# A hybrid decoder layer on one core: gMLP and twelve column tiles moved to the front, there in pairs of seven block products

## The chip, the core and the metric

The kernel runs on one core of one Trainium2 chip. TensorE (PE) multiplies matrices into PSUM banks; VectorE (DVE), ScalarE (ACT) and GpSimd (POOL) work element by element; SyncE (SP) issues most of the DMAs, ScalarE some. Each engine works off its own instructions in the order of the program and waits at semaphores. The metric is the device time of one execution in microseconds; the kernel before takes 1228.83 us (median of 3 runs, 1227.72 to 1228.85).

## The reference, cut to what matters

x is 1024 tokens by 1024 channels, float32. Every mixer has four heads or groups, 256 channels wide.

```python
h = rmsnorm(x, norm_gain)
proj = h @ w_in                       # all inputs of all mixers and the merge gates
ys = (gated_deltanet(gdn_qkv, ..., gdn_z, ...),
      spatial_gating(sg_u, sg_v, sg_z, ...),       # gMLP
      rwkv7_time_mix(rw, rw_z, ...),
      native_sparse_attention(nsa_q, nsa_kv, ..., nsa_z, ...))
gates = jnp.split(jax.nn.sigmoid(merge), 4, axis=-1)
mixed = sum(gates[i] * (ys[i] @ w_branch[i]) for i in range(4))
return rmsnorm(x + mixed @ w_out, final_gain)
# in spatial_gating: u, v = gelu(u), gelu(v); v = layernorm over 64 channels;
# mixed = lower-triangular 128x128 position mixing of v per group; u * (mixed + b) * silu(z)
```

## The kernel before

The input projection is cut into column tiles of 128 output channels. The normalised input lies in SBUF as two parts, hh (rounded) and hl (the rest), all 1024 channels by 1024 tokens, with channels on partitions. A weight tile is loaded in two halves (wt, L1001), and each is split into wh (ScalarE, L1006) and wl (VectorE, L1008). A column tile (`col_tile`) has two halves of 512 tokens; for each, 8 steps over the channels by 3 products (hh·wh, hh·wl, hl·wh: L1023 to L1025), 24 matmuls a half and 48 a tile. The result leaves PSUM through ScalarE (L1034, or L1051 for a gate) and is parked in DRAM. These are called dense matmuls here.

The program is traced in this order: a first stage (rmsnorm, mixed with the tiles RW 6, 2, 3), the tiles RW 0, 1, 4, 5 and RWZ, a small projection (L1181 on), the rwkv mixer, tiles GD and GDZ, the gated delta mixer (`gdn`), tiles NK, NQ, NZ, the sparse attention (`nsa`), tiles GM 2, 3, 0, 1 and GMZ (gMLP's inputs and gate), the gMLP mixer (`gmlp`, L617), the 32 tiles of the merge gates, the merge (L1256 to L1258) and the output projection (L1287 to L1290) with the last norm. A scheduler at build time fixes each engine's order: work traced later fills the places where work traced earlier would wait, so column tiles that are traced behind a mixer stand between its instructions. Weight splits have high priority.

The mixers' results Y are read back from DRAM before the merge: sixteen loads (yr, L1236, two buffers), each split into yh (ScalarE, L1237) and yl (VectorE, L1238), in the order Y2, Y0, Y3, Y1 (rwkv, delta, attention, gMLP). Beside them the weights of the output projection are loaded (wot, L1223, two buffers) and split on ScalarE and POOL (L1225). The pool of these buffers shares SBUF space with the attention's pools.

gMLP works on halves of 512 tokens: gelu of v (VectorE L612 and L614), 16 transposes (L655), a layernorm (L660 to L667, with a power on POOL, L667), gelu of u (L612 on POOL), the scale (L676), 64 matmuls for the position mixing (L683), and two products (L685, L689).

Of the kernel before, what the change touches and what calls it, by code (L numbers as in the profile page):

```python
# [19 lines left out]
D = 1024  # L20
# [596 lines left out]
def gmlp(G, src, zs, y, ws, bs, lg, lb):  # L617
# [3 lines left out]
    with tc.tile_pool(name="gm", bufs=1, reuse_waits="tile") as P:  # L621
# [17 lines left out]
        def front(half):  # L639
# [4 lines left out]
            t = P.tile([128, 4, 512], F32, name="gmt")  # L644
# [3 lines left out]
            gelu2(nc, x[:, 2:4], t[:, 2:4], nc.vector.tensor_mul)  # L648
# [19 lines left out]
            gelu2(nc, x[:, 0:2], t[:, 0:2], nc.gpsimd.tensor_mul)  # L668
# [314 lines left out]
def body(tc, xT, x, w, wsm, rw_up, rw_cols, gd_conv, gd_hp, gd_gw, gm_ws, gm_bs, gm_lg, gm_lb,  # L983
# [4 lines left out]
    with ExitStack() as ctx:  # L988
        G = setup(tc, ctx)
        hpool = ctx.enter_context(tc.tile_pool(name="h", bufs=1))  # L990
        sp = ctx.enter_context(tc.tile_pool(name="stream", bufs=1))
# [7 lines left out]
        def load_w(src, k0, n):  # L999
            wt = sp.tile([128, 4, 128], F32, name="wt", bufs=3)  # L1000
            nc.sync.dma_start(wt[:, :, :n], src[:, k0:k0 + 4])  # L1001
            return wt

        def split_w(wt, eng=nc.gpsimd, pool=sp, bufs=3):
            wh = pool.tile([128, 4, 128], F32R, name="wh", bufs=bufs)
            nc.scalar.copy(wh, wt)  # L1006
            wl = pool.tile([128, 4, 128], F32R, name="wl", bufs=bufs)
            eng.tensor_sub(wl, wt, wh.bitcast(F32))  # L1008
            return wh, wl
# [18 lines left out]
        def stage():  # L1028
            return sp.tile([128, 512], F32, name="stg", bufs=4)
# [39 lines left out]
        with tc.tile_pool(name="xp", bufs=1) as XP:  # L1069
            banks = [[bank(G, tag, n) for _ in range(2)] for tag, n in (("st", 2), ("m", 2), ("sc", 3))]  # L1070

            def load_x(pc, a):
                if a == 0:
                    xs[pc] = XP.tile([128, 8, 256], F32, name="xt", bufs=3)
                ks = slice(4 * a, 4 * a + 4)
                nc.sync.dma_start(xs[pc][:, ks], xT.rearrange("k p t -> p k t")[:, ks, 256 * pc:256 * pc + 256])

            def stats(pc):

                xt = xs[pc]  # L1080
                s2 = XP.tile([128, 8, 256], F32, name="xsq", bufs=2)
                for a in range(2):
                    ks = slice(4 * a, 4 * a + 4)
                    nc.scalar.activation(s2[:, ks], xt[:, ks], AF.Square)
                    nc.vector.tensor_add(s2[:, 4 * a:4 * a + 2], s2[:, 4 * a:4 * a + 2], s2[:, 4 * a + 2:4 * a + 4])
                nc.vector.tensor_add(s2[:, 0:2], s2[:, 0:2], s2[:, 4:6])
                pss = bank(G, "sc", 3) if pc == 2 else bank(G, "acc", 1)
                for t in range(2):
                    for k in range(2):
                        nc.tensor.matmul(pss[:, t:t + 1], s2[:, k, 128 * t:128 * t + 128], one, start=(k == 0), stop=(k == 1))  # L1090
                rs = XP.tile([128, 2], F32, name="xrs", bufs=2)
                nc.vector.tensor_scalar(rs, pss[:, 0:2], 1.0 / D, 1e-6, op0=OP.mult, op1=OP.add)
                nc.gpsimd.tensor_tensor(rs, rs, G.mhalf[:, 0:2], op=OP.pow)
                return rs, pss[:, 256:512]

            def spread(rs, pb):

                with tc.issue_after(after.ins):
                    for t in range(2):
                        nc.tensor.transpose(pb[:, 128 * t:128 * t + 128], rs[:, t:t + 1].to_broadcast([128, 128]), G.ident)  # L1100
                return pb

            def apply(pc, rb):
                xt, sl = xs[pc], slice(256 * pc, 256 * pc + 256)
                for k in range(8):
                    nc.vector.scalar_tensor_tensor(xt[:, k], xt[:, k], gn[:, k:k + 1], rb, op0=OP.mult, op1=OP.mult)
                    nc.scalar.copy(hh[:, k, sl], xt[:, k])
                    (nc.gpsimd if k % 3 == 1 else nc.vector).tensor_sub(hl[:, k, sl], xt[:, k], hh[:, k, sl].bitcast(F32))

            def products(pc, ks, j, parts):  # L1110
                sl = slice(256 * pc, 256 * pc + 256)
                p = banks[j][pc // 2][:, 256 * (pc % 2):256 * (pc % 2) + 256]
                for k in ks:
                    wh, wl = w0[j][k // 4]
                    for n in parts:
                        a, b = ((wh, hh), (wh, hl), (wl, hh))[n]
# [256 lines left out]
```

## Time and profile before

| | us |
|---|---|
| median of the runs | 1228.83 |
| the profiled execution | 1225.36 |
| its span in the trace | 1223.6 |
| TensorE busy in it | 1168.8 (96%) |
| VectorE | 816.5 (67%) |
| ScalarE | 539.0 (44%) |
| GpSimd | 176.8 (14%) |

The span is the traced execution from its first to its last instruction, on the profile's own clock; the execution's device time has a little around it. Engines overlap, so the shares are not a sum. Matmuls are pipelined: one is listed with some 0.4 us, but the next starts after 0.23 us. Some matmul records are missing from the trace.

### The profile page before, as it was taken

The numbers are of one execution on the slowest core, as the hardware profiler recorded it, in microseconds if no ns is written. First come the engines' busy times: TensorE is split into PE (matmuls) and PEld (weight loads), VectorE is DVE, ScalarE is ACT, GpSimd is POOL, SyncE is SP. The second block draws the span as 40 slices with busy tenths as digits, with TensorE's granted clock in tenths as the row PEclk, the third lists the DMA queues.
The fourth block names the chain that finished last, engine by engine and source line by source line (L and its number), as shares of the span: only waits on it lengthen the run. The fifth ranks groups of instructions, "written<-read, shape, count | busy, mean of one in ns | idle before, by whom it ended". The sixth has DMA issues, their size and how long they took to land. (4 is left out here: it accounts for less than half of the span.)

```text
span 1223.6 us, 18178 instructions
## 1 busy us (share of the span) xinstructions
PE 1168.8 (96%) x6214; PEld 948.3 (78%) x6214; DVE 816.5 (67%) x2309; ACT 539.0 (44%) x1366; POOL 176.8 (14%) x158
## 2 busy tenths in 40 slices
PE   7999999998999999989999999999999999999997
PEld 6888777786777777877777887777787778888886
DVE  7612699778574868969765798888867431788122
ACT  6422454454333465575554565556554342221222
POOL 5320000100002000001000000000003220675510
PEclk9999999999999999999999999999999999999999
DMA  6222443121322553323323322212125563676223
GB/s 219 78 103 86 145 133 118 61 74 35 108 79 70 121 170 99 105 82 102 110 80 126 127 78 65 66 52 69 45 69 189 180 225 112 230 243 216 95 86 129
DMA packets 113105, 140.11 MB, mean 115 GB/s; under 512 B 36544, under 2 KB 59968, under 8 KB 112884
## 3 DMA queue, kind: packets, MB, share of 16 engines
q1 hardware_dynamic: 95588, 107.22, 27.9%
q10 hardware_dynamic: 17424, 31.73, 7.1%
q8 instruction: 49, 0.80, 0.3%
q14 instruction: 44, 0.36, 0.1%
HBM read 94.78 MB, written 44.12 MB: 114 GB/s over the span
## 5 line engine op out<-in xcount | busy, mean ns | idle before, releaser
L1023 PE MATMUL st<-hh,wh 128*128 128x512 f32 x944 | 380.4, 403 | 2.3 <-ACT stg L1051 2.3
L1024 PE MATMUL st<-hh,wl 128*128 128x512 f32 x944 | 379.4, 402 | 0.0
L1025 PE MATMUL st<-hl,wh 128*128 128x512 f32 x944 | 377.2, 400 | 0.0
L1023 PEld LDWEIGHTS st<-hh,wh 128*128 128x128 f32 x944 | 178.7, 189 | 35.9 <-ACT stg L1051 3.6
L1025 PEld LDWEIGHTS st<-hl,wh 128*128 128x128 f32 x944 | 178.4, 189 | 32.7 <-issue 1.0
L1024 PEld LDWEIGHTS st<-hh,wl 128*128 128x128 f32 x944 | 178.5, 189 | 32.3 <-issue 1.9
L1008 DVE TENSOR_TENSOR wl<-wt,wh 128x512 fp32r<-128x512 f32 x134 | 99.0, 740 | 96.4 <-ACT wh L1006 94.3
L1006 ACT CAST wh<-wt 128x512 fp32r<-128x512 f32 x140 | 86.3, 618 | 113.3 <-PE st L1025 103.8
L917 ACT ACTIVATE P<-sc,m 128x512 f32<-128x512 f32 (+3 forms) x80 | 44.8, 563 | 30.7 <-DVE m L912 19.5
L1051 ACT ACTIVATE stg<-st 128x512 f32<-128x512 f32 x64 | 38.1, 595 | 41.6 <-PE st L1025 41.4
L102 DVE TENSOR_TENSOR invP<-invX,invL 128x16 f32<-128x16 f32 (+18 forms) x240 | 53.9, 259 | 0.3
L105 DVE TENSOR_REDUCE invX<-invP 128x8 f32<-128x240 f32 (+18 forms) x240 | 52.7, 252 | 0.2
L1287 PE MATMUL sc<-woh,hh 128*128 128x512 f32 x128 | 49.8, 389 | 0.0
L1288 PE MATMUL sc<-wol,hh 128*128 128x512 f32 x128 | 49.8, 389 | 0.0
L1293 DVE TENSOR_TENSOR o<-sc,xr 128x512 f32<-128x512 f32 x16 | 11.1, 692 | 56.1 <-PE sc L1290 56.1
L1264 POOL TENSOR_TENSOR mx<-mx,stg 128x512 f32<-128x512 f32 x28 | 38.6, 1379 | 60.2 <-DVE stg L1263 59.1
L912 DVE TENSOR_REDUCE m<-sc 128x1 f32<-128x512 f32 (+3 forms) x80 | 41.2, 532 | 0.6 <-PE sc L837 0.2
L1034 ACT COPY stg<-st 128x512 f32<-128x512 f32 x39 | 22.9, 587 | 39.9 <-PE st L1025 35.7
L1270 ACT CAST hh<-mx 128x512 fp32r<-128x512 f32 x16 | 9.9, 622 | 62.6 <-POOL mx L1264 54.8
L30 POOL IOTA tril<- 128x128 f32 x1 | 0.2, 248 | 234.6 <-PE sc L837 234.6
L259 POOL MEMSET sv<- 64x512 f32 x8 | 4.2, 519 | 201.0 <-ACT O L297 162.4
L1295 ACT ACTIVATE jk<-o 128x512 f32<-128x512 f32 x16 | 10.1, 631 | 51.6 <-DVE o L1293 51.6
(458 smaller groups left out, 2386.7 us busy)
## 6 DMA issues: line engine op xcount, KB each, us to landing
wt<-in_w_dram SPq DMA_DIRECT2D x124, 256.0 KB, 2.8
gate<-stg ACTq DMA_DIRECT2D x64, 256.0 KB, 2.2
gt<-gate SPq DMA_DIRECT2D x32, 256.0 KB, 3.3
stg<-gate SPq DMA_DIRECT2D x32, 256.0 KB, 3.2
xt<-in_xT_dram SPq DMA_DIRECT2D x8, 512.0 KB, 7.4
wot<-in_wo_dram SPq DMA_DIRECT2D x16, 256.0 KB, 3.0
wt<-in_wb_dram SPq DMA_DIRECT2D x16, 256.0 KB, 3.1
xr<-in_x_dram SPq DMA_DIRECT2D x16, 256.0 KB, 2.6
```

Of the source, the lines that this page charges most:

```text
L102: nc.vector.tensor_mul(prv[:, rs, :, :m], X[:, rs, None, c:].to_broadcast(d), L[:, None, c:c + 2, c:].to_broadcast(d))
L105: nc.vector.tensor_reduce(X[:, rs, c:c + 2], prv[:, rs, :, :m], axis=AX.X, op=OP.add)
L912: nc.vector.tensor_reduce(m2[:, h, gi:gi + 1], pz[:, :n], axis=AX.X, op=OP.max, negate=True)
L917: nc.scalar.activation(Pt[gi][:, h, :n], pp[gi][:, :n], AF.Exp, bias=m2[:, h, 0:1], accum_out=ss[:, gi, h:h + 1])
L1006: nc.scalar.copy(wh, wt)
L1008: eng.tensor_sub(wl, wt, wh.bitcast(F32))
L1023: nc.tensor.matmul(p, wh[:, kk], hh[:, k, sl], start=(k == 0), stop=False)
L1024: nc.tensor.matmul(p, wl[:, kk], hh[:, k, sl], start=False, stop=False)
L1025: nc.tensor.matmul(p, wh[:, kk], hl[:, k, sl], start=False, stop=(k == 7))
L1264: (nc.vector if j == 7 else nc.gpsimd).tensor_add(mx, mx, g)
L1287: nc.tensor.matmul(p, mh[:, k, ts], a[:, k], start=(k == 0), stop=False)
L1288: nc.tensor.matmul(p, mh[:, k, ts], b[:, k], start=False, stop=False)
```

## The change

1. In the front, behind RW 0 and 1, six pairs of column tiles are computed with seven products of blocks where a pair of plain tiles has eight: GM(2,3), GM(0,1), GMZ, then RW(4,5), RWZ, GD(2,3). A pair is a 2 by 2 block product: two column tiles by two halves of the channels by two halves of the tokens, each product 4 steps by 3 matmuls. It needs sums of weight blocks (VectorE) and four differences of blocks of the input (fh, fl, computed once on VectorE and ScalarE from the input tiles xt, which now stay). Some sums of products are accumulated in one PSUM bank (cc), others are made by VectorE. The seventh product of a pair is issued within the next pair (`rest`).
2. `gmlp` is traced behind the first three pairs and no longer behind `nsa`; its work tile gmt has half the size.
3. The weight buffers are 7 (wt), 4 (wh, wl) and 6 (stg) in the front, and 3, 3 and 4 behind it, as before.

```diff
-            t = P.tile([128, 4, 512], F32, name="gmt")
+            t = P.tile([128, 2, 512], F32, name="gmt")
...
+          for h in range(2):
+              xa, xb, lo, hi = xs[h], xs[2 + h], slice(0, 4), slice(4, 8)
...
+              def part(r, v, sl=sl):
+                  nc.scalar.copy(fh[r][:, :, sl], v)
+                  nc.vector.tensor_sub(fl[r][:, :, sl], v, fh[r][:, :, sl].bitcast(F32))
+
+              nc.vector.tensor_sub(xa[:, lo], xa[:, lo], xb[:, lo])
+              part(0, xa[:, lo])
+              nc.vector.tensor_sub(xb[:, lo], xb[:, hi], xb[:, lo])
+              part(2, xb[:, lo])
+              nc.vector.scalar_tensor_tensor(xb[:, hi], xa[:, lo], -1.0, xb[:, hi], op0=OP.mult, op1=OP.subtract)
+              part(1, xb[:, hi])
+              nc.vector.scalar_tensor_tensor(xa[:, hi], xb[:, hi], -1.0, xa[:, hi], op0=OP.mult, op1=OP.subtract)
+              part(3, xa[:, hi])
...
+        def col_pair(col, dst, keep, rest):
...
+            def product(p, f, r, ks, sl, new):
+                wh, wl = f
+                for k in range(4):
...
+                    nc.tensor.matmul(p, wh[:, k], m, start=new and k == 0, stop=False, **chk)
+                    nc.tensor.matmul(p, wl[:, k], m, start=False, stop=False, **chk)
+                    nc.tensor.matmul(p, wh[:, k], l, start=False, stop=(k == 3), **chk)
+
+            with tc.high_priority():
+                s = load_s()
+                nc.vector.tensor_add(s, a, c)
+                nc.vector.tensor_add(c, c, d)
+            product(y, factor(c), 0, 0, None, True)
+            m5 = stage()
+            with tc.high_priority():
+                nc.scalar.activation(m5, y, AF.Copy, scale=-1.0)
+            if rest:
+                rest()
+            product(cc, factor(a), None, 0, t0, True)
+            m1 = stage()
+            with tc.high_priority():
+                nc.scalar.copy(m1, cc)
+                nc.vector.tensor_add(a, a, c)
+            product(x, factor(b), None, 4, t0, True)
+            with tc.high_priority():
+                nc.vector.tensor_add(m1, x, m1)
+            keep(m1, dst[0], t0)
+            product(cc, factor(a), 1, 0, None, False)
...
+            product(y, factor(b), None, 4, t1, False)
+            with tc.high_priority():
+                nc.vector.tensor_add(u2, y, u2)
+            keep(u2, dst[0], t1)
+            product(cc, factor(s), 2, 0, None, False)
+            with tc.high_priority():
+                nc.vector.scalar_tensor_tensor(m5, cc, -1.0, m5, op0=OP.mult, op1=OP.add)
+            keep(m5, dst[1], t1)
+            fd = factor(d)
+
+            def rest():
+                product(cc, fd, 3, 0, None, False)
...
-        for i in (0, 1, 4, 5):
+        for i in (0, 1):
             col_tile(C_RW + i, park(rwd[i]))
-        for i in range(2):
-            col_tile(C_RWZ + i, park_silu(Z[2][i]))
+        rest = None
+        for i in (2, 0):
+            rest = col_pair(C_GM + i, gmd[i:i + 2], keep, rest)
+        col_pair(C_GMZ, Z[1], keep_silu, rest)()
+        gmlp(G, gmd, Z[1], Y[1], gm_ws, gm_bs, gm_lg, gm_lb)
+        rest = col_pair(C_RW + 4, rwd[4:6], keep, None)
+        rest = col_pair(C_RWZ, Z[2], keep_silu, rest)
+        rest = col_pair(C_GD + 2, gdd[2:4], keep, rest)
+        rest()
```

The plain tiles of GM, GMZ and GD 2, 3 and the call of `gmlp` are gone from their old places. TensorE has 5436 instructions in place of 5508. In the program after, matmuls of column tiles are L1025 to L1027, of pairs L1222 to L1224, of the merge L1359 to L1361; the loads yr are L1339, those of output weights L1326.

On SP's queue the loads yr, near the end of the attention; before (y__102 is gMLP's result, y__103 that of rwkv):

```order
L690 DMA y__102<-gmy 128x512 x2
L1001 DMA wt<-in_w_dram 128x512
L690 DMA y__102<-gmy 128x512 x2
L1001 DMA wt<-in_w_dram 128x512
L1236 DMA yr<-y__103 128x512 x2
L1223 DMA wot<-in_wo_dram 128x512 x2
L1251 DMA gt<-gate_120 128x512
```

and after (y__104 is the attention's result):

```order
L972 DMA y__104<-yt 128x128 x2
L1003 DMA wt<-in_w_dram 128x512
L1003 DMA wt<-in_wb_dram 128x512 x2
L1326 DMA wot<-in_wo_dram 128x512 x2
L972 DMA y__104<-yt 128x128 x2
L1326 DMA wot<-in_wo_dram 128x512
L1339 DMA yr<-y__103 128x512 x2
L1326 DMA wot<-in_wo_dram 128x512
L1354 DMA gt<-gate_120 128x512
```

The first loads yr stood behind gMLP's last stores; now they stand behind the attention's last store and a load of output weights.

On TensorE the passage from the last column tile to the merge, before (500 dense matmuls and gMLP's stand between it and the attention's last matmul):

```order
L1024 MATMUL st<-hh,wl 128x512
L1025 MATMUL st<-hl,wh 128x512
L1256 MATMUL sc<-yh_8558,wh 128x512
L1257 MATMUL sc<-yh_8558,wl 128x512
L1258 MATMUL sc<-yl_8566,wh 128x512
```

and after, 82 dense matmuls behind it (yh_8644 and 8645 are the delta mixer's, 8648 and 8649 rwkv's):

```order
L1026 MATMUL st<-hh,wl 128x512
L1027 MATMUL st<-hl,wh 128x512
L1359 MATMUL sc<-yh_8644,wh 128x512
L1360 MATMUL sc<-yh_8644,wl 128x512
L1361 MATMUL sc<-yl_8652,wh 128x512
L1359 MATMUL sc<-yh_8648,wh 128x512
```

The merge stands 418 dense matmuls closer to the attention's end; its first thirty matmuls need the delta mixer's and rwkv's results only.

On TensorE in the front, gMLP's first transposes and the end of the pair GMZ, which have no counterpart there before (fh_707 is the fourth difference, st the bank cc, sc the bank of the next pair RW(4,5)):

```order
L1224 MATMUL st<-fl_710,wh 128x512
L636 MATMUL m<-gmw,gml 64x128 x4
L655 MATMUL m<-ident,gmx 128x128 x4
L1222 MATMUL sc<-fh_704,wh 128x512
L1222 MATMUL st<-fh_707,wh 128x512
L1223 MATMUL st<-fh_707,wl 128x512
```

gMLP's transposes stand within the pairs, ahead of GMZ's seventh product (the last two rows and ten more).

## Rows read from the trace of the kernel before

**Rows 1.** The page: busy time by engine, and one of the costliest groups.

```profile
PE 1168.8 (96%) x6214; PEld 948.3 (78%) x6214; DVE 816.5 (67%) x2309; ACT 539.0 (44%) x1366; POOL 176.8 (14%) x158
...
L1006 ACT CAST wh<-wt 128x512 fp32r<-128x512 f32 x140 | 86.3, 618 | 113.3 <-PE st L1025 103.8
```

**Rows 2.** Busy time of each engine in stretches; start and end, length first.

```profile
core 0: us, PE busy (x) PEld busy (x) DVE busy (x) ACT busy (x) POOL busy (x), PEclk, DMA share, GB/s
60.00:82.00 22.00, 22.00 (x99) 18.22 (x98) 2.77 (x4) 4.78 (x9) 10.13 (x10) 1.00 0.27 95
922.00:945.00 23.00, 20.94 (x101) 17.23 (x100) 20.45 (x27) 13.39 (x18) 9.04 (x3) 1.00 0.49 167
945.00:966.00 21.00, 17.43 (x113) 13.23 (x112) 13.40 (x22) 3.48 (x6) 3.33 (x2) 0.92 0.33 114
966.00:1010.00 44.00, 41.68 (x182) 33.55 (x181) 15.71 (x22) 21.31 (x38) 11.28 (x8) 1.00 0.72 239
...
1042.00:1216.00 174.00, 174.00 (x769) 144.14 (x768) 90.57 (x129) 38.86 (x76) 85.18 (x65) 1.00 0.51 172
1216.00:1223.60 7.60, 0.40 (x2) 0.00 (x0) 1.66 (x3) 1.44 (x3) 0.55 (x1) 0.70 0.22 88
```

**Rows 3.** Timeline of TensorE: start, listed length, line and tile.

```profile
910.10 0.40 PE L937 MATMUL acc<-plo,VS 128*128 128x512 f32 x1
...
943.64 0.39 PE L1023 MATMUL st<-hh,wh 128*128 128x512 f32 x1
943.87 0.39 PE L1024 MATMUL st<-hh,wl 128*128 128x512 f32 x1
...
945.68 0.39 PE L1023 MATMUL st<-hh,wh 128*128 128x512 f32 x1
...
1042.15 0.39 PE L1256 MATMUL sc<-yh,wh 128*128 128x512 f32 x1
```

**Rows 4.** The chain of waits that ended last, from 900 to 1060 us.

```profile
954.38 0.66 PE m L683 x8
...
976.66 5.72 DMA yr<-y__101
```

**Rows 5.** A stretch of two microseconds in gMLP; columns as in rows 2.

```profile
956.00:958.00 2.00, 2.00 (x7) 1.62 (x6) 0.70 (x2) 0.00 (x0) 0.00 (x0) 0.56 0.54 200
```

**Rows 6.** Groups on VectorE from 922 to 966 us: busy, mean ns, idle before.

```profile
L1008 DVE TENSOR_TENSOR wl<-wt,wh 128x512 fp32r<-128x512 f32 x6 | 4.1, 689 | 3.5 <-ACT wh L1006 3.5
```

**Rows 7.** Timelines of VectorE and then of POOL in gMLP.

```profile
923.56 1.23 DVE L612 TENSOR_TENSOR gmt<-gmt,gmx 128x1024 f32<-128x1024 f32 x1
...
926.31 3.14 DVE L614 SCALAR_TENSOR_TENSOR gmx<-gmt,gmx 128x1024 f32<-128x1024 f32 x1 [0.17 <-ACT gmt L613]
...
938.50 1.22 DVE L614 SCALAR_TENSOR_TENSOR gmx<-gmt,gmx 128x1024 f32<-128x1024 f32 x1
...
925.68 2.69 POOL L612 TENSOR_TENSOR gmt<-gmt,gmx 128x1024 f32<-128x1024 f32 x1 [29.96 <-DMA gmx<-gmd]
938.65 3.92 POOL L612 TENSOR_TENSOR gmt<-gmt,gmx 128x1024 f32<-128x1024 f32 x1 [10.28 <-DVE gms L666]
```

**Rows 8.** Timeline of SP's queue: stores of the attention, loads yr.

```profile
912.48 0.33 SPq L972 DMA_DIRECT2D y__104<-yt  x1
...
964.73 0.45 SPq L1236 DMA_DIRECT2D yr<-y__103  x1
```

**Rows 9.** Lines L1237, L1238, L1225: ns min/median/max; landing of yr; timeline of VectorE.

```profile
L1237 ACT CAST yh<-yr x16: 612/620/626, 969.6 to 1008.2; 128x512 fp32r<-128x512 f32 x16
...
L1238 DVE TENSOR_TENSOR yl<-yr,yh x16: 685/693/876, 970.3 to 1008.9; 128x512 fp32r<-128x512 f32 x16
...
L1225 POOL TENSOR_TENSOR wol<-wot,woh x16: 1278/1295/1806, 971.4 to 1152.5; 128x512 fp32r<-128x512 f32 x16
...
DMA to landing us min/median/max: 2.6/3.4/5.7
...
1004.80 0.69 DVE L1238 TENSOR_TENSOR yl<-yr,yh 128x512 fp32r<-128x512 f32 x1 [1.81 <-ACT yh L1237]
```

More of the change, by code (lines that the diff above doesn't have):

```diff
@@ L647, in front @@
                 nc.sync.dma_start(z[:, p], zs[p][:, t0:t0 + 512])
-            gelu2(nc, x[:, 2:4], t[:, 2:4], nc.vector.tensor_mul)
+            gelu2(nc, x[:, 2:4], t, nc.vector.tensor_mul)
             vt = P.tile([128, 4, 4, 64], F32, name="gmv", bufs=2)
@@ L1028, in stage @@
         def stage():
-            return sp.tile([128, 512], F32, name="stg", bufs=4)
+            return sp.tile([128, 512], F32, name="stg", bufs=nbufs["stg"])
         def park(dst):
@@ new lines, in keep, with keep_silu, factor @@
+        def keep(s, dst, sl):
+            nc.scalar.dma_start(dst[:, sl], s)
+        def keep_silu(s, dst, sl):
+            t = stage()
+            nc.scalar.activation(t, s, AF.Tanh, scale=0.5)
+            nc.vector.scalar_tensor_tensor(s, t, 1.0, s, op0=OP.add, op1=OP.mult)
+            nc.scalar.dma_start(dst[:, sl], s)
+        def col_pair(col, dst, keep, rest):
+            t0, t1 = slice(0, 512), slice(512, 1024)
+            c, d = (load_w(w[col + 1], 4 * kh, 128) for kh in range(2))
+            a, b = (load_w(w[col], 4 * kh, 128) for kh in range(2))
+            cc, x, y = bank(G, "st", 2), bank(G, "sc", 3), bank(G, "sc", 3)
+            def factor(wt):
+                with tc.high_priority():
+                    return split_w(wt, nc.vector)
+            def product(p, f, r, ks, sl, new):
+                wh, wl = f
+                for k in range(4):
+                    m, l = (fh[r][:, k], fl[r][:, k]) if r is not None else (hh[:, ks + k, sl], hl[:, ks + k, sl])
+                    chk = dict(skip_group_check=not new)
+                    nc.tensor.matmul(p, wh[:, k], m, start=new and k == 0, stop=False, **chk)
[21 more added lines that the diff above has]
+            product(cc, factor(a), 1, 0, None, False)
+            u2 = stage()
+            with tc.high_priority():
+                nc.scalar.copy(u2, cc)
+                nc.vector.tensor_add(b, b, a)
+            product(y, factor(b), None, 4, t1, False)
+            with tc.high_priority():
+                nc.vector.tensor_add(u2, y, u2)
+            keep(u2, dst[0], t1)
+            product(cc, factor(s), 2, 0, None, False)
+            with tc.high_priority():
+                nc.vector.scalar_tensor_tensor(m5, cc, -1.0, m5, op0=OP.mult, op1=OP.add)
[3 more added lines that the diff above has]
+                product(cc, fd, 3, 0, None, False)
+                s = stage()
+                nc.scalar.activation(s, cc, AF.Copy, scale=-1.0)
+                keep(s, dst[1], t0)
+            return rest
@@ L1176, in body @@
+        rest = col_pair(C_GD + 2, gdd[2:4], keep, rest)
+        rest()
+        first_stage.close()
+        sp = ctx.enter_context(tc.tile_pool(name="stream", bufs=1, reuse_waits="tile"))
+        nbufs = dict(wt=3, wh=3, stg=4)
         with tc.tile_pool(name="sm", bufs=1, reuse_waits="tile") as SM:
@@ L1195, in body @@
         rwkv(G, rwd, Z[2], Y[2], rw_up, rw_cols)
-        for i in (2, 3, 0, 1, 4, 5):
+        for i in (0, 1, 4, 5):
             col_tile(C_GD + i, park(gdd[i]))
```

213 lines of the change are left out of this document (109 added, 104 removed).

## The prediction, made before the changed kernel ran

> **What bounds the kernel now.** I read the page's shares first: TensorE is busy 96% of the span, VectorE and ScalarE wait for TensorE's results most of the time they wait at all (the cast of a weight tile sat idle 103.8 us behind the last matmul of a tile) [rows 1]. Then the stages. In a stretch of plain column tiles (60 to 82 us) TensorE has no idle time and VectorE works 2.8 of 22 us [rows 2]. The pitch of the dense matmuls is read from their starts: 943.64 and 943.87 us, 0.2268 us over a longer run of them (943.64 to 945.68, nine steps) [rows 3]. So a dense matmul taken away from such a stretch is worth 0.227 us, and one that is only moved is worth nothing, unless there was idle time that it covered or will cover. Idle time there is in two places that this change touches: the gMLP stretch (922 to 966 us, TensorE busy 38.4 of 44) and what follows it; from 1042 us to 1216 us there is none [rows 2].
>
> **What goes.** The program after has 72 dense matmuls fewer: six pairs of column tiles at 84 in place of 96. 72 x 0.227 = 16.3 us. The gMLP stretch at the end goes too. Between the last matmul of the fourth mixer (910.10 us) and the first of the merge (1042.15 us) [rows 3] lie 132.0 us, with 500 dense matmuls (113.4 us) and gMLP's own: 64 of L683 at 0.66 us for 8 [rows 4], 5.3 us, and some 1.9 us for its transposes (estimate, 16 larger ones and two more at a pitch like that). The rest, 11.4 us, is waiting and matmuls at the lower clock: TensorE waits for VectorE in gMLP, and behind those waits the granted clock is 0.56 for a while, that is near 1.2 GHz [rows 5].
>
> **What is moved to the front.** Counted up to the last matmul of the fourth mixer, the order has 346 dense matmuls more than before (504 in pairs against fewer single tiles later): 78.5 us. gMLP's matmuls add 7.2. If nothing else happened, that matmul would come at 910.1 + 78.5 + 7.2 = 995.8 us. The fillers that stand between the mixers' own steps are about as many as before (692, 813 and 529 dense matmuls in the three later mixers' stretches, against 653, 827 and 520), so I cost the mixers at nothing, give or take 5 us; the rwkv mixer still begins behind the small projection with 45 dense matmuls as cover.
>
> In the front, a pair costs 84 x 0.227 = 19.1 us of TensorE. VectorE has to do seven low parts (L1008's operation, 0.69 us undisturbed [rows 6]), four sums of weights and three sums out of PSUM, all of 128x512; the nearest row has 0.69 us for each, so 14 x 0.69 = 9.7 us, and for the two gated pairs 2.8 more. Single pairs are therefore covered by TensorE. gMLP isn't: VectorE was busy 33.85 us in 922 to 966 us [rows 2], of which six low parts of weights took 4.1 [rows 6], so gMLP takes 29.7. It now stands beside the pairs RW(4,5) and RWZ: 2 x 9.7 + 2.8 + 29.7 = 51.9 us of VectorE against 38.2 + 7.2 = 45.4 us of TensorE. The excess, 6.5 us, is what TensorE waits if nothing can be shifted out of these two pairs, 0 if the neighbours take all of it (GD(2,3) has 9 us of slack, but weights can be prepared only four splits ahead). Besides, the seventh product of the gates' pair now waits for a sum that VectorE has queued behind gMLP's STT L614, and gMLP's own chains (VectorE to POOL and back) stay. I take **s = 5 us** for all waits in front, with 0 and 12 as the ends: 0 if the fillers cover the chains, 12 if the excess and the gMLP waits of before (5.6 us idle in 922 to 966 [rows 2]) simply add.
>
> The sixteen new VectorE and eight new ScalarE operations that make the four differences of x (128x1024; the nearest row has 1.22 us [rows 7], 19.5 us in all) lie beside the two plain tiles RW 0 and 1, 96 x 0.227 = 21.8 us, so they cost nothing; without that cover 3 us.
>
> **What is late next: the loads of the mixers' results.** The sixteen loads yr (L1236) stand on SP's queue behind the last store of the fourth mixer, now as before, and are two buffers deep. Before, they could begin at 964.73 us only, and took until the fifteenth low part ended at 1004.80 + 0.69 us [rows 8, 9], 40.8 us; it cost nothing, because gate tiles were left until 1042 us. After, only 82 dense matmuls are left behind the mixer (18.6 us) and 36 merge matmuls that need early loads (8.2 us), 26.8 us in all.
>
> The start: the store stood 2.4 us behind the last matmul (912.48 [rows 8] less 910.10). In the new order a load of output weights stands between it and the first yr, and waits for POOL's L1225, which waits for a cast behind ten further matmuls: 2.3 + 0.6 + 0.6 + 1.3 [rows 9] + 0.4 for issue = 5.2 us. From there 40.8 us at the old pace. If a load takes its median, 3.4 us, and the cast 0.62 and the low part 0.69 [rows 9], a step is 4.7 us and the eight take 37.6: the old pace was set beside gate stores and loads at a DMA share of 0.72 [rows 2], of which fewer are left, while one load took 5.72 us there [rows 4]. I take 39.3, between them: the fifteenth part is ready 44.5 us behind the mixer's last matmul (ends 42.8 and 46.0). TensorE idles 44.5 - 26.8 = 17.7 us, in two pieces. After waits that long the clock will come back late, as at 956 to 958 us, where seven matmul records stand in 2 us at 0.56 [rows 5]; I add 2 us (ends 0 and 3).
>
> **The sum.** 995.8 + 5 + 44.5 + 2, then 768 - 36 = 732 matmuls of merge and output projection at 0.2268 (166.0 us), then 7.4 us as in the last window [rows 2]: 1220.7 us of span, against 1223.6. That is 2.9 us less. In other words: 16.3 us of matmuls and 11.4 us of old waits go, 19.7 us of new wait behind the last mixer and 5 us in front come. The profiled execution took 1225.36 us, 1.8 beyond its span, and lies 3.5 below the median of the runs, 1228.83; I take the difference over to the median: **1226 us**.
>
> **A rule against it.** The row first: an L614, which takes 1.22 us elsewhere, took 3.14 us when it began at 926.31, just after POOL's L612 (925.68, 2.69 us); and the second L612 took 3.92 us when VectorE's L614 had begun ahead of it [rows 7]. So VectorE lost 1.9 us to one POOL instruction. The Trainium skill, "SBUF — State Buffer", section "Who interferes with whom", says that a VectorE instruction with two SBUF inputs and a GpSimd instruction that reads SBUF exclude each other for a whole instruction; the trace agrees, for L614 ended 1.1 us behind POOL's instruction. Beside the pairs VectorE is full of such instructions (weight sums, low parts), where before it mostly had time.
>
> **Rivals.**
> 1. *The front hides all* (s = 0, yr at 42.8, clock 2): 995.8 + 42.8 + 2 + 173.4 = 1214.0, 9.6 us less, **1219 us**. For it: VectorE's total in front, some 95 us beside 121 us of TensorE; against it: the two pairs with gMLP.
> 2. *VectorE becomes the bound in front.* Its queue is in order, and every product needs a low part from it. With s = 12, yr at the old pace (46.0) and clock 3, 995.8 + 12 + 46.0 + 3 + 173.4 = 1230.2, 6.6 us more, **1235 us**. It decides against the change from s = 8 on with the rest as forecast. For it: 51.9 against 45.4 us; against it: the slack before and behind.
> 3. *The exclusion between POOL and VectorE repeats in front.* Two L612 (2.69 and 3.92 us) blocking VectorE whole for up to 2.7 us each, where VectorE is already the longer one, make s = 5 + 2 x 1.9 = 8.8 by the row above: 1224.5 of span, 0.9 us more, **1230 us**: no change that can be told.
>
> That the change doesn't do what it says I exclude: the order has the 72 matmuls less.
>
> **Chances.** Forecast 0.40, rival 1 0.25, rival 2 0.22, rival 3 0.13. The forecast's own range is 1222 to 1230, from the ends of pace and clock with s between 3 and 8. What a measurement can tell here is about 0.2%, 2.5 us. Faster than 1226.4: rival 1 and just over half of the forecast, 0.47. Slower than 1231.3: rival 2 and a little of rival 3, 0.25. Between: 0.28. The range that should hold eight in ten is 1213 to 1238: rival 1 with the mixers 5 us shorter, rival 2 with a little more than its 12 us.
>
> **What would show it.** Right: TensorE without idle from the first stage to the gates' pair; a few microseconds of waits for VectorE beside gMLP; the last matmul of L937's kind (L939 after) near 1000 us; then 18 us of dense matmuls, two gaps of together some 18 us ended by the yr chain, a granted clock near a half behind them. Wrong: gaps in front over 10 us; a merge that starts without a gap; mixers whose stretches grow by more than 5 us beyond their matmuls.

## The result: slower by 1.2%, and the profile after

The changed kernel takes 1242.8 us (median of 4 runs, 1241.71 to 1243.56) against 1228.84 us of the kernel before; the ratio is 1.0118 (95% interval 1.0098 to 1.0137). The prediction was 1226 us with a range up to 1238: it was wrong, in the sign and beyond the range. The profiled execution took 1243.44 us, with a span of 1241.6.

The page of the changed kernel: busy time by engine, and from the 40 slices those of TensorE and of its granted clock.

```profile
PE 1169.8 (94%) x6142; PEld 942.4 (76%) x6142; DVE 874.7 (70%) x2385; ACT 558.7 (45%) x1392; POOL 176.4 (14%) x158
...
PE   7899998999999989999999999999999996899997
...
PEclk9899998999999999999999999999999999899999
```

TensorE has 72 instructions fewer, yet as many busy microseconds as before (1169.8 against 1168.8 [rows 1]), and its share falls from 96% to 94%. Both say the same: more waiting, and more time at the lower clock (the mean granted clock is 0.982, 0.995 before). The digits show where both lines fall: slices 2, 7, 34 and 35.

Stretches of the changed kernel; columns as in [rows 2].

```profile
32.00:48.00 16.00, 13.12 (x88) 12.43 (x87) 11.72 (x27) 5.48 (x13) 2.97 (x4) 0.79 0.23 84
60.00:207.00 147.00, 145.33 (x688) 116.71 (x687) 107.12 (x151) 63.32 (x100) 13.53 (x6) 1.00 0.34 120
207.00:220.00 13.00, 7.77 (x26) 4.33 (x25) 2.96 (x6) 3.03 (x5) 7.16 (x6) 0.74 0.47 129
1036.00:1066.00 30.00, 16.80 (x51) 11.78 (x52) 14.30 (x21) 10.12 (x18) 3.82 (x4) 0.77 0.63 211
1066.00:1100.00 34.00, 30.62 (x125) 23.98 (x124) 23.73 (x34) 6.67 (x12) 26.78 (x20) 0.95 0.64 210
```

The pairs themselves (60 to 207 us) keep TensorE busy for 145.3 of 147 us. The loss is around them: in the first stage (32 to 48), at the seam between the pairs and the next mixer (207 to 220, 7.8 of 13 us) and behind the attention (1036 to 1066, 16.8 of 30, where before gate tiles filled the time to 1042 and [rows 2] shows no idle time after it).

By events in the two profiled executions, with dense matmuls counted from the order and priced at 0.2268 us:

| stretch | before, us | after, us | dense matmuls more | lost beyond them and gMLP's 7.2 us |
|---|---|---|---|---|
| start to the first stage's last matmul | 55.4 | 60.1 | -4 | 5.6 |
| from there to the first rwkv product (L277) | 97.4 | 187.7 | 316 | 11.4 |
| from there to the attention's last matmul | 757.3 | 769.0 | 34 | 4.0 |
| from there to the end | 313.5 | 224.8 | -418 | 13.3 (24.6 idle or at the lower clock, 11.3 before) |

The losses are 34.3 us; less the 16.3 us of the 72 matmuls that makes the 18.0 us by which the span grew. Between the medians it is 14.0 us: the profiled execution of the kernel before lies 3.5 us below its median, that of the changed kernel 0.6 above. So some 4 us of the table belong to the choice of executions, and the row of the mixers (4.0 us) is of that size; the part on why the prediction was wrong comes back to it.

### The seam

Timeline of the changed kernel from TensorE, POOL, SP and VectorE, in this order: the last pair's last matmul, the small projection's first, and what it waited for.

```profile
207.69 0.39 PE L1224 MATMUL st<-fl,wh 128*128 128x512 f32 x1
213.31 0.69 PE L1296 MATMUL st<-hh,ws 128*64 128x512 f32 x1 [5.23 <-DVE ws L1290]
...
208.15 0.53 POOL L1287 MEMSET wz<- 128x512 f32 x1 [38.12 <-PE st L1224]
...
208.70 0.68 SPq L1288 DMA_DIRECT2D wz<-in_wsm_dram  x1
...
211.78 0.43 DVE L1289 CAST ws<-wz 128x512 fp32r<-128x512 f32 x1 [6.81 <-DMA wz<-in_wsm_dram]
...
212.94 0.32 DVE L1290 TENSOR_TENSOR ws<-wz,ws 128x160 fp32r<-128x160 f32 x1
```

The space of wz, the small projection's weights, was held by the front's pools until the last pair's last matmul at 207.69. Only then does POOL clear it (208.15), SP load it (208.70), VectorE cast and subtract (211.78 and 212.94), and TensorE starts at 213.31. TensorE waits 5.2 us, and its next matmuls are at the lower level: 0.74 is the mean of the stretch. Before, the same projection followed the plain tiles without a wait:

```profile
119.51 0.39 PE L1025 MATMUL st<-hl,wh 128*128 128x512 f32 x1
119.73 0.40 PE L1188 MATMUL st<-hh,ws 128*64 128x512 f32 x1
```

### The first stage

VectorE in the changed kernel, from 29 to 36 us; L1089 and L1090 are the sums for the statistics of the third block of tokens, L1096 their end. The last line is the end of the fourth block's.

```profile
29.51 0.68 DVE L1089 TENSOR_TENSOR xsq<-xsq 128x512 f32<-128x512 f32 x1
31.09 1.29 DVE L1010 TENSOR_TENSOR wl<-wt,wh 128x512 fp32r<-128x512 f32 x2 [0.89 <-ACT wh L1008]
32.30 0.69 DVE L1089 TENSOR_TENSOR xsq<-xsq 128x512 f32<-128x512 f32 x1
32.90 0.69 DVE L1228 TENSOR_TENSOR wt<-wt 128x512 f32<-128x512 f32 x1
33.50 0.68 DVE L1090 TENSOR_TENSOR xsq<-xsq 128x512 f32<-128x512 f32 x1
34.10 0.68 DVE L1229 TENSOR_TENSOR wt<-wt 128x512 f32<-128x512 f32 x1
35.80 0.16 DVE L1096 TENSOR_SCALAR xrs<-sc 128x2 f32<-128x2 f32 x1 [1.02 <-PE sc L1094]
...
48.38 0.16 DVE L1096 TENSOR_SCALAR xrs<-acc 128x2 f32<-128x2 f32 x1 [2.75 <-PE acc L1094]
```

The third block's end in the kernel before, and its stretch from 32 to 48 us.

```profile
28.84 0.69 DVE L1086 TENSOR_TENSOR xsq<-xsq 128x512 f32<-128x512 f32 x1
...
31.59 0.16 DVE L1092 TENSOR_SCALAR xrs<-sc 128x2 f32<-128x2 f32 x1 [0.81 <-PE sc L1090]
...
32.00:48.00 16.00, 14.90 (x115) 14.00 (x115) 13.83 (x34) 8.99 (x21) 6.01 (x8) 1.00 0.16 60
```

Low parts (L1010) and weight sums of the first pair (L1228, L1229) stand between the sums of the statistics, whose end comes at 35.80 in place of 31.59 us. Up to 62 us TensorE waits 3.0 us for what POOL makes of the statistics (1.0 before) and 1.1 us for the sums (0.2 before), and it works at a granted clock of 0.79 over the 16 us (1.00 before).

### Behind the attention

Timeline of TensorE, SP and VectorE, in this order, behind the attention's last matmul (1016.77): the merge's matmuls that waited, some loads, and the fifteenth low part.

```profile
1016.77 0.42 PE L937 MATMUL acc<-plo,VS 128*128 128x512 f32 x1
...
1036.78 0.50 PE L1359 MATMUL sc<-yh,wh 128*128 128x512 f32 x1 [0.97 <-ACT yh L1340]
...
1043.76 0.79 PE L1359 MATMUL sc<-yh,wh 128*128 128x512 f32 x1 [2.94 <-ACT yh L1340]
...
1058.46 0.79 PE L1359 MATMUL st<-yh,wh 128*128 128x512 f32 x1 [8.89 <-ACT yh L1340]
...
1087.32 0.50 PE L1359 MATMUL st<-yh,wh 128*128 128x512 f32 x1 [2.09 <-DVE stg L1366]
...
1022.41 0.90 SPq L1339 DMA_DIRECT2D yr<-y__103  x2
...
1055.21 5.35 SPq L1339 DMA_DIRECT2D yr<-y__102  x4
1066.27 0.32 SPq L1354 DMA_DIRECT2D stg<-gate  x1
...
1062.38 0.69 DVE L1341 TENSOR_TENSOR yl<-yr,yh 128x512 fp32r<-128x512 f32 x1 [2.17 <-ACT yh L1340]
```

This is the wait that the prediction had named. The first yr was issued 5.6 us behind the last matmul (1022.41) and the fifteenth low part ended 46.3 us behind it (1063.07), near the end of 46.0 in the sum. TensorE waited 2.9 and 8.9 us, and the first matmul behind either takes 0.79 us as listed, 0.39 otherwise. It did not wait for the fifteenth low part: it went on at 1058.46, 41.7 us behind the last matmul, when the thirteenth load was cast (ScalarE, 1057.79 and 0.62 us). The sum had not seen two later waits (1.1 and 2.1 us), for VectorE's L1366, which works on the loaded gates. The next gate load (L1354) stands behind the yr on SP's queue and begins at 1066.27, when POOL's L1367 has set its buffer free.

### The profile page after: what moved, and what is told of

It is laid out like the page before. It is cut to its first block, busy times and chain, and to the rows that moved or that the text cites. A ratio compares the mean times of both kernels' runs of the same rounds, so it can differ in the third digit from the quotient of the medians.

```text
span 1241.6 us, 18127 instructions
## 1 busy us (share of the span) xinstructions
PE 1169.8 (94%) x6142; PEld 942.4 (76%) x6142; DVE 874.7 (70%) x2385; ACT 558.7 (45%) x1392; POOL 176.4 (14%) x158
## 4 chain that ended last, share of the span: by engine, by line
PE 68%; DVE 13%; DMA 6%; ACT 6%; issue 4%; POOL 3%; SPq 0%; POOLq 0%; DVEq 0%; ACTq 0%
PE st L1026 9%; PE st L1027 9%; PE st L1025 9%; PE sc L1393 2%; PE sc L1390 2%; PE sc L1391 2%; PE st L1222 1%; PE st L1223 1%; PE st L1224 1%; DVE wl L1010 1%; PE sc L836 1%; PE acc L936 1%; DVE invX L105 1%; PE sc L1223 1%; DVE invP L102 1%
## 5 line engine op out<-in xcount | busy, mean ns | idle before, releaser
L1027 PE MATMUL st<-hl,wh 128*128 128x512 f32 x752 | 304.3, 405 | 0.0
L1026 PE MATMUL st<-hh,wl 128*128 128x512 f32 x752 | 303.6, 404 | 0.0
L1025 PE MATMUL st<-hh,wh 128*128 128x512 f32 x752 | 302.9, 403 | 0.0
L1027 PEld LDWEIGHTS st<-hl,wh 128*128 128x128 f32 x752 | 142.5, 190 | 25.2 <-issue 1.6
L1026 PEld LDWEIGHTS st<-hh,wl 128*128 128x128 f32 x752 | 142.7, 190 | 24.8 <-issue 0.8
L1025 PEld LDWEIGHTS st<-hh,wh 128*128 128x128 f32 x752 | 142.6, 190 | 24.0 <-issue 0.2
L1010 DVE TENSOR_TENSOR wl<-wt,wh 128x512 fp32r<-128x512 f32 x152 | 110.9, 731 | 69.8 <-ACT wh L1008 68.1
L102 DVE TENSOR_TENSOR invP<-invX,invL 128x16 f32<-128x16 f32 (+19 forms) x240 | 53.9, 257 | 0.3
L105 DVE TENSOR_REDUCE invX<-invP 128x8 f32<-128x240 f32 (+19 forms) x240 | 51.7, 250 | 0.2
L1367 POOL TENSOR_TENSOR mx<-mx,stg 128x512 f32<-128x512 f32 x28 | 38.1, 1365 | 28.6 <-DVE stg L1366 27.3
L1359 PE MATMUL st<-yh,wh 128*128 128x512 f32 x64 | 26.9, 421 | 12.3 <-ACT yh L1340 8.9
L1398 ACT ACTIVATE jk<-o 128x512 f32<-128x512 f32 x16 | 10.1, 631 | 51.7 <-DVE o L1396 51.7
L468 DVE SCALAR_TENSOR_TENSOR cvt<-graw,cw,cvt 128x256 f32<-128x256 f32 x72 | 31.7, 476 | 0.2
```

The source lines that it names most:

```text
L102: nc.vector.tensor_mul(prv[:, rs, :, :m], X[:, rs, None, c:].to_broadcast(d), L[:, None, c:c + 2, c:].to_broadcast(d))
L105: nc.vector.tensor_reduce(X[:, rs, c:c + 2], prv[:, rs, :, :m], axis=AX.X, op=OP.add)
L1025: nc.tensor.matmul(p, wh[:, kk], hh[:, k, sl], start=(k == 0), stop=False)
L1026: nc.tensor.matmul(p, wl[:, kk], hh[:, k, sl], start=False, stop=False)
L1027: nc.tensor.matmul(p, wh[:, kk], hl[:, k, sl], start=False, stop=(k == 7))
```

## The experiments

Ratios are to the kernel before, timed on the same chip, with 95% intervals. The theory after the result: three separate waits (seam, first stage, yr chain), each with a stretch at the lower clock behind it, and the pairs themselves sound. Rivals: VectorE's work in the pairs eats their gain; or the waits only move when one is taken away.

**The pairs alone.** `e7_plain`: plain tiles at the pairs' places, and no fh and fl.

```diff
...
-        for i in (2, 0):
-            rest = col_pair(C_GM + i, gmd[i:i + 2], keep, rest)
-        col_pair(C_GMZ, Z[1], keep_silu, rest)()
+        for i in (2, 3, 0, 1):
+            col_tile(C_GM + i, park(gmd[i]))
+        for i in range(2):
+            col_tile(C_GMZ + i, park_silu(Z[1][i]))
...
```

> The changed kernel with plain column tiles (eight products, 48 matmuls a tile) in the places of the six pairs, and without the differences fh and fl. Theory (the pairs themselves bring what their matmuls say, the loss is in the move): the front has 72 matmuls more, 16.3 us, less the waits for VectorE in the pairs (1.7 us), the slower pitch of products on fh and fl (about 2 us) and some of the wait at the seam, since the blocks that hold it up are gone: 1250 to 1257. Rival (VectorE's work for the pairs costs the front as much as the matmuls save): 1243 or less.

1253.64 us, ratio 1.0199 (1.0173 to 1.0225), against 1.0118 with pairs: the pairs bring 0.8%, some 10 us of their 16.3. The first rwkv product comes at 258.2 us against 247.8. The rival falls: the pairs gain, and the rest of the change costs more than they gain.

**The yr chain.** `e3_yr4`:

```diff
-                            yr = M.tile([128, 512], F32, name="yr", bufs=2)
+                            yr = M.tile([128, 512], F32, name="yr", bufs=4)
```

> Four buffers in place of two for the loads yr. Theory (the chain load, cast, low part, next load, two deep, sets the tail): the eight steps of some 5 us become about four, the wait of 8.9 us before gMLP's part and that of 2.9 us before it nearly go, with part of the half clock behind them: 10 to 14 us less, 1229 to 1233. Rival (the DMA engines, at a share of 0.7 there, set the pace of the loads): sixteen loads take as long as now, under 4 us gained, 1239 or more.

1231.97 us, ratio 1.0034 (1.0013 to 1.0055): 0.8% less, 10 us. Stretches as above:

```profile
1036.00:1066.00 30.00, 23.79 (x91) 17.40 (x90) 21.38 (x29) 11.10 (x20) 16.54 (x12) 0.94 0.85 285
1066.00:1100.00 34.00, 34.00 (x152) 28.15 (x151) 27.70 (x39) 7.24 (x13) 27.40 (x19) 1.00 0.79 252
```

TensorE is busy 23.8 of 30 us in place of 16.8, and without a gap from 1066. The last of the sixteen loads is issued 20.3 us behind the first (1022.27 and 1042.58), in place of 37.8 us (1022.41 and 1060.24). The depth of the chain had set the tail, not the DMA engines, whose share rose to 0.85.

**The seam, first try.** `e1_seam`: the pool of ws and wz opens behind gMLP; the projection's matmuls come before the front's pools close.

```diff
+        SM = first_stage.enter_context(tc.tile_pool(name="sm", bufs=1, reuse_waits="tile"))
+        ws = SM.tile([128, 8, 2, 32], F32R, name="ws")
...
         rest()
+        for th in range(2):
...
+                    nc.tensor.matmul(p[0:64], ws[:, k].rearrange("q a c -> q (a c)"), hx[:, k, sl],
...
         first_stage.close()
```

> The weights of the small projection (ws, wz) get a place that the pairs' blocks do not hold: their pool is opened behind gMLP, and the projection's matmuls are traced before the front's pools close. Theory (the wait at the seam is the release of the pairs' space): TensorE's 5.2 us wait at L1296 goes, and with it the half clock from 212 to 218 us (some 2 us): 7 us less than the changed kernel's 1242.8, so 1236. Rival (the release is only met one step later, by the rwkv mixer's own tiles): the wait turns up before rwkv's first matmuls, gain under 2 us, 1241 or more.

1247.55 us, ratio 1.0152 (1.0135 to 1.0168): slower still. TensorE's waits from 200 to 250 us (total, times, longest), and SP's queue there:

```profile
PE st L1025 <- ACT wh L1008: 10.1, 1, 10.1
```

```profile
217.36 3.95 SPq L1298 DMA_DIRECT2D smd<-stg  x2
...
223.44 8.49 SPq L1003 DMA_DIRECT2D wt<-in_w_dram  x5
```

The wait for ws is gone, and one of 10.1 us for the first weight tile of the new pool has come: its loads stand at 223.44, behind the projection's two stores and rwkv's loads. The rwkv product comes at 247.9 us, as without the edit, but with 39 dense matmuls fewer done by then (646 for 685 behind the first stage), which is 8.8 us of work. The rival was right: taken away in one place, the wait came back at the next. What holds these loads in the trace is their place on SP's queue; that the closing of the pool puts them there is argued from `e10_one` below, where no pool of weights is closed: its weight loads go on during the projection (210.69 and 214.61 us), and no such wait is left.

**Is it the pool?** `e5_before_bufs`: the kernel before with the front's pool of 7, 4 and 6 buffers, closed behind RWZ. `e6_before_x4`: the kernel before with four xt buffers. One execution of each.

```diff
+        sp = first_stage.enter_context(tc.tile_pool(name="stream0", bufs=1))
+        nbufs = dict(wt=7, wh=4, stg=6)
...
+        first_stage.close()
+        sp = ctx.enter_context(tc.tile_pool(name="stream", bufs=1, reuse_waits="tile"))
+        nbufs = dict(wt=3, wh=3, stg=4)
```

```diff
-                    xs[pc] = XP.tile([128, 8, 256], F32, name="xt", bufs=3)
+                    xs[pc] = XP.tile([128, 8, 256], F32, name="xt", bufs=4)
```

> The kernel before with one edit: the front's weight pool has 7, 4 and 6 buffers (closed behind RWZ, then 3, 3 and 4 again). Theory (the buffers let weight work run ahead of the first stage's statistics): the first stage's last matmul, at 55.4 us before and 60.1 in the changed kernel, comes at 59 us or later. Rival (it is the four xt buffers, by which x is loaded in another order): it stays within a microsecond of 55.4.

> The kernel before with one edit: four buffers for the blocks of x (xt) in place of three. Theory (the weight buffers make the first stage late): its last matmul within a microsecond of 55.4 us. Rival (the four xt buffers make it late): 58.5 us or later.

1242.85 us for the first, without a pair or a moved gMLP, beside runs of the kernel before at 1230.38 (median); 1230.36 for the second, no change. In the first, TensorE waits at the seam:

```profile
PE st L1193 <- DVE ws L1187: 6.9, 1, 6.9
```

Its first rwkv product comes at 164.3 us against 152.8: 11.5 us, 2.1 of them in the first stage (last matmul 57.5 us), 7.3 from there to the projection, 2.1 behind it. So the loss at the seam needs nothing of the change but its pools. Of the first stage's loss the pools alone make some 2 us: 57.5 lies between what the theory (59 or later) and the rival (within 1 us of 55.4) said. With four xt buffers the first stage ends at 54.6: they are innocent by themselves.

**The first stage alone.** `e2_first`: splits of RW 1 and of the first pair may stand on VectorE only behind the last statistics (a handle kept in `stats`).

```diff
...
+        col_tile(C_RW, park(rwd[0]))
         rest = None
...
+        with tc.issue_after(late["dve"].ins):
+            col_tile(C_RW + 1, park(rwd[1]))
+            rest = col_pair(C_GM + 2, gmd[2:4], keep, rest)
+        rest = col_pair(C_GM, gmd[0:2], keep, rest)
```

> The weight splits of RW 1 and the weight sums and splits of the first pair may stand on VectorE only behind the last statistics of the first stage. Theory (weight work of high priority, for which the front's seven and four buffers leave room, runs ahead of the statistics of the third token block and holds up the first stage): the first stage's last matmul comes near 55.5 us in place of 60.1, the granted clock stays at 1 from 36 to 44 us, 4 to 5 us less, 1238. Rival (the first stage is late because more loads of weights share the DMA engines with x): the third block is as late as before, under 1 us gained, 1242 or more.

1245.31 us, ratio 1.0133 (1.0108 to 1.0159): no gain. The third block's statistics end 2.0 us earlier than in the changed kernel, the fourth's 3.2 us (VectorE's timeline; lines are one further down, L1111 is the normalisation of a block):

```profile
33.82 0.16 DVE L1097 TENSOR_SCALAR xrs<-sc 128x2 f32<-128x2 f32 x1 [0.65 <-PE sc L1095]
...
45.19 0.16 DVE L1097 TENSOR_SCALAR xrs<-acc 128x2 f32<-128x2 f32 x1 [3.33 <-PE acc L1095]
45.33 0.69 DVE L1229 TENSOR_TENSOR wt<-wt 128x512 f32<-128x512 f32 x1
45.93 1.29 DVE L1010 TENSOR_TENSOR wl<-wt,wh 128x512 fp32r<-128x512 f32 x2
...
47.74 1.26 DVE L1111 SCALAR_TENSOR_TENSOR xt<-xt,gains,acc 128x256 f32<-128x256 f32 x3
```

The work that was held back now stands right behind the last statistics, ahead of the last block's normalisation, and the stage ends 13.8 us behind these statistics in place of 11.7: at 59.0 us, not at 55.5. Nor is that a gain over 60.1, for `e1_seam`, `e3_yr4` and `e8_warm`, whose edits lie elsewhere, end the stage at 61.4, 59.3 and 59.1. So weight work did stand in the way of the statistics, and the edit put it in the way of what follows them. The rival, loads of x held up by loads of weights, fits no better: they land in 8.6 us (median) in the changed kernel and 7.4 before, but in 4.5 in `e5_before_bufs` (end at 57.5) and 8.6 in `e11_three` (end at 56.5). With the same buffers and no pairs (`e7_plain`) the stage ends at 57.9, with pairs and fewer buffers (`e10_one`) at 57.3: as far as single executions tell, buffers and pairs each cost it some 2 us. By what steps stays open.

**The clock.** `e8_warm`: matmuls nobody reads in TensorE's waits.

```diff
+        def idle(n, ins):
+            with tc.issue_after(ins):
+                p = bank(G)
+                for k in range(n):
+                    nc.tensor.matmul(p, hh[:, 0, 0:128], hh[:, 1, 0:512], start=(k == 0), stop=(k == n - 1))
...
-        rest()
+        idle(23, rest().ins)
...
+                idle(70, ins.ins)
```

> The changed kernel with matmuls whose result nobody reads where TensorE waits: 23 behind the last pair (5.2 us, as long as the wait for ws) and 70 behind the last gate tile (15.9 us). Nothing else is changed, so work is only added. Theory (a good part of the loss is the half clock behind each wait): the granted clock stays near 1 from 212 to 220 us and from 1044 to 1064 us, and the time falls by 3 to 7 us, to 1236 to 1240. Rival (the chains of loads set the time whatever the clock): no change within 1.5 us, or slower.

1243.16 us, ratio 1.0119 (1.0083 to 1.0155): no difference that can be measured. Stretches at the seam and in the tail:

```profile
207.00:220.00 13.00, 12.63 (x56) 8.68 (x55) 3.38 (x6) 3.04 (x5) 6.36 (x5) 1.00 0.49 129
1048.00:1066.00 18.00, 12.47 (x39) 9.20 (x38) 7.39 (x12) 3.95 (x7) 3.86 (x3) 0.72 0.37 119
```

At the seam the clock stays at 1, and from the projection's first matmul to rwkv's first product 32.4 us pass in place of 34.5: 2.1 us. In the tail the first merge matmuls only came later (1048.0), TensorE still waited 4.5 us for yh, and the clock fell as before: nothing gained. TensorE went on behind that wait 40.8 us after the attention's last matmul, 41.7 us in the changed kernel. So the half clock was worth about 2 us at the seam, and behind the attention the chain of loads set when TensorE went on; what the slow matmuls behind its waits cost there, this run can't tell.

**Two attempts at a better kernel.** `e4_all`: the edits of `e1_seam`, `e2_first` and `e3_yr4` together.

> The three edits together (small projection's place, weight work behind the first statistics, four yr buffers). Theory (three separate new waits, each with a stretch of half clock behind it): the gains add, 7 + 4.5 + 12 = 23 us, 1219 to 1221, that is 8 to 10 us below the kernel before. Rival (what is gained in one place is given back in the mixers or by VectorE in the pairs): over 1228.

1227.14 us, ratio 1.0000 (0.998 to 1.0021): between the theory and the rival: what the yr buffers bring and some 4 us, not the sum, for neither of the other edits had gained anything alone.

`e10_one`: one weight pool for the whole kernel, as in the kernel before, of 5, 3 and 4 buffers.

```diff
-        sp = first_stage.enter_context(tc.tile_pool(name="stream0", bufs=1))
-        nbufs = dict(wt=7, wh=4, stg=6)
+        sp = ctx.enter_context(tc.tile_pool(name="stream", bufs=1))
+        nbufs = dict(wt=5, wh=3, stg=4)
...
-        sp = ctx.enter_context(tc.tile_pool(name="stream", bufs=1, reuse_waits="tile"))
-        nbufs = dict(wt=3, wh=3, stg=4)
```

> The changed kernel with one weight pool from the start to the end, 5 wt, 3 wh and wl, 4 stg, in place of a front pool of 7, 4 and 6 that is closed behind the last pair and a new one of 3, 3 and 4. Theory (the closing of the front's pool makes the wait at the seam, and its buffers let weight work run ahead in the first stage): the wait for ws goes with the half clock behind it (7 us), the first stage ends 3 us earlier: 1231 to 1235. Rival (the pairs need the buffers): five and three buffers starve the pairs, and the front's last pair ends no earlier than now, at 207 us or later, 1239 or more.

1236.39 us, ratio 1.0068 (1.0047 to 1.0088): 0.5% less than the change, some 6 us; the wait at the seam is gone, the first stage ends at 57.3 us. A little less than expected, and the rival was right in part: the last pair ends at 212.8 us in place of 207.7. Beside the pairs, TensorE waits 3.8 us for gMLP's VectorE work where the changed kernel waits 0.6, and the clock falls:

```profile
170.00:180.00 10.00, 6.57 (x55) 4.68 (x56) 5.75 (x11) 0.00 (x0) 4.48 (x1) 0.84 0.34 126
```

With four yr buffers as well (`e9_one543`), and with six (`e12_yr6`):

> As the kernel with one weight pool, and four yr buffers. Theory (seam, first stage and yr chain are three separate losses that add): 1220 to 1225, below the kernel before. Rival (some of it is given back): 1229 or more.

> One weight pool and six yr buffers in place of four. With four, the stretch from the first merge matmul to the end is still 8.5 us longer than before, with waits for yh, yl and the merge's weights. Theory (part of that is still the depth of the yr loads): the last loads come some 3 us earlier, 1219 to 1222. Rival (the loads are now at the pace of the transfers and of what else stands in the queues): within 1.5 us of the 1223 with four buffers.

1223.05 us, ratio 0.9965 (0.9949 to 0.998), and 1223.03 us, 0.9948 (0.993 to 0.9965): both below the kernel before; six buffers add nothing clear. Stretches of the first of them, seam and tail:

```profile
204.00:224.00 20.00, 20.00 (x87) 14.35 (x86) 6.58 (x18) 4.93 (x9) 2.08 (x4) 1.00 0.45 137
1030.00:1060.00 30.00, 24.54 (x96) 18.18 (x95) 22.09 (x29) 12.34 (x22) 16.93 (x13) 0.94 0.81 272
```

**The cover kept.** `e11_three`: one pool, two yr buffers, pairs for RW(4,5), RWZ and GD(2,3) only; gMLP and its plain tiles at their old place.

```diff
-        for i in (2, 0):
-            rest = col_pair(C_GM + i, gmd[i:i + 2], keep, rest)
-        col_pair(C_GMZ, Z[1], keep_silu, rest)()
-        gmlp(G, gmd, Z[1], Y[1], gm_ws, gm_bs, gm_lg, gm_lb)
...
+            for i in (2, 3, 0, 1):
+                col_tile(C_GM + i, park(gmd[i]))
...
```

> One weight pool (5, 3, 4), two yr buffers; pairs for RW(4,5), RWZ and GD(2,3) only, in the front; gMLP and its tiles, as plain tiles, at their old place behind the attention. So 36 matmuls less than before and the old cover of the yr loads. Theory (the loss of the change lies in the move of gMLP and of the uncovered dense work, which took the cover from the yr loads, and in the pools, not in the pairs): 36 x 0.227 = 8 us less than before, less some 2 us for the pairs' waits: 1220 to 1224. Rival (the pairs cost in front what they save): 1228 or more.

1224.4 us, ratio 0.9971 (0.9955 to 0.9986), at the edge of what was expected: half the pairs, and no change to the yr loads, give as much as all six with four yr buffers. Its stretch from the first merge matmul to the end is 181.2 us, as before (181.4), where the change has 204.8.

## Why the prediction was wrong, point by point

- **The 72 matmuls** (16.3 us): right in number. Alone they bring some 10 us (e7). Products on the new blocks fh and fl start every 0.2333 us, not 0.2268: 288 x 0.0065 = 1.9 us. Waits in the pairs are 1.7 us.
- **"I take s = 5 us for all waits in front"**: the failed step. The front lost 17.0 us (the table's 5.6 and 11.4), over the 12 that the prediction gave as the end for all waits there. And it lost them elsewhere. Beside gMLP, where I had put the 5 us, TensorE waits 0.3 and 0.6 us (and 0.8 in the last pair): VectorE's 51.9 against 45.4 us were worked off in the slack before and behind. What I had costed at nothing cost the most. One part is the seam, "the rwkv mixer still begins behind the small projection with 45 dense matmuls as cover", when the projection itself had to wait for the space of the front's pools: 5.2 us, and 2.1 at half clock by e8. With the waits in the pairs and their slower products that makes 10.9 of the 11.4 us. e5 shows that the pools do this without the rest of the change, and e10 that it goes when no pool of weights is closed. The other part is the first stage, where I had costed only the new differences (which start at 59.28 us and cost TensorE nothing: it is busy for 20.0 of the 20 us from 60 to 80). It lost 5.6 us in this execution; some 2 us come with the buffers alone (e5), and the rest stays open.
- **The mixers "at nothing, give or take 5 us"**: not shown to be wrong. The table has 4.0 us over their matmuls, but `e5_before_bufs` and `e6_before_x4`, whose TensorE order from the first rwkv product on is that of the kernel before, took 761.1 and 762.2 us up to the attention's last matmul, where the profiled execution of the kernel before took 757.3. In the attention (from the first L778 to the last L937) the changed kernel took 238.3 us, with a granted clock of 0.56 to 0.58 from 804 to 812 us; `e8_warm` and `e9_one543`, with the same order there, took 235.3 and 235.4.
- **What is late next: the loads yr**: right in mechanism and place, and e3 shows it. Their pace was the old one: 40.7 us from the first issue to the fifteenth low part, where the sum had 39.3 and the kernel before 40.8. Sharing DMA engines was no reason for a faster one, for with four buffers the loads went faster at a higher share. The sum has 36 merge matmuls as cover where the order shows thirty, and thirty ran before the wait of 8.9 us. The term that was mis-sized is the clock: idle and half clock together are 24.6 us (224.8 less 850 matmuls at 0.2268 and 7.4 at the end) for 19.7, of which the waits listed are 16.8 us for 17.7, and the slow matmuls behind them 7.8 us for the 2 (ends 0 and 3) that I had added.
- **Rival 2** had the right sign, by the wrong mechanism: VectorE isn't the bound in the pairs. **Rival 3**: the exclusion is there and costs little. POOL's L612 and the low parts that fell beside it (timelines of the changed kernel, POOL and then VectorE):

```profile
131.60 2.77 POOL L612 TENSOR_TENSOR gmt<-gmt,gmx 128x1024 f32<-128x1024 f32 x1 [58.23 <-DVE gmt L611]
...
162.06 2.72 POOL L612 TENSOR_TENSOR gmt<-gmt,gmx 128x1024 f32<-128x1024 f32 x1 [2.74 <-DVE gmt L611]
...
133.00 1.92 DVE L1010 TENSOR_TENSOR wl<-wt,wh 128x512 fp32r<-128x512 f32 x1 [0.89 <-ACT wh L1008]
...
162.45 0.68 DVE L662 TENSOR_TENSOR gmv<-m,gms 128x512 f32<-128x512 f32 x1
163.85 1.49 DVE L1010 TENSOR_TENSOR wl<-wt,wh 128x512 fp32r<-128x512 f32 x1 [0.71 <-ACT wh L1008]
```

A low part of 0.69 us took 1.92 and 1.49 us, until some 0.55 us behind POOL's end, while L662, with one input in PSUM, took its 0.68. That is 2.0 us of VectorE where the rival had 3.8; TensorE's next wait behind the first came at 139.08 us and was 0.3 us. The Trainium skill, "SBUF — State Buffer", section "Who interferes with whom", says that a VectorE instruction with two inputs in SBUF contends with a GpSimd instruction that reads SBUF, and that one with at most one input in SBUF, outside the two-port modes, does not; the trace agrees in both points.
- **The sum**: 1220.7 us of span predicted, 1241.6 measured: 12 us from the front, 4 from the mixers, 4.9 from the tail. Between the medians, 1226 and 1242.8, it is 16.8 us: the other 4.1 us are the 3.5 that the forecast took over from the profiled execution of the kernel before, and 0.6 of the changed kernel's.

## What to carry to other kernels

Closing a pool costs at the seam what the next users of its space need to get going (clear, load, cast, subtract: here 5.2 us, then some 2 us at half clock), unless something that doesn't need the space stands there: list for each pool that closes who gets its place and what covers them. More buffers and a high priority can let work run ahead into a stage that is itself critical (some 2 us of the first stage in e5, one execution). And dense work that covers nothing where it stands may be the cover of a chain of loads two stages on: deepen that chain before moving it.

## What the runs showed of the hardware that was not expected

The pitch of matmuls of one shape differs with the tile that they read, at a granted clock of 1.00. In the first pair the starts of products of twelve matmuls each (TensorE's timeline):

```profile
81.80 0.39 PE L1222 MATMUL sc<-fh,wh 128*128 128x512 f32 x1
...
84.60 0.39 PE L1222 MATMUL st<-hh,wh 128*128 128x512 f32 x1
...
87.34 0.39 PE L1222 MATMUL sc<-hh,wh 128*128 128x512 f32 x1
```

That is 0.2333 us a step on fh and fl and 0.2283 on hh and hl right behind them; the second product on hh and hl in a row ends at 90.06, 0.2267 a step, as in plain tiles (0.2268). Why is not shown.

After a wait of 5.2 us the granted clock of 207 to 220 us is 0.74, and with matmuls nobody reads in that wait it is 1.00; waits of 0.3 to 0.8 us in the pairs left it at 1.00.
